# Own buffers for modulation tiles, a four-block start of an output projection, and moved gates in a two-layer hybrid decoder

## The chip, the cores and the metric

The kernel runs on one core of one Trainium2 chip. The metric is the device time of one execution in microseconds, the median of several runs. The engines are TensorE (PE: matmuls; PEld: their weight loads), VectorE (DVE), ScalarE (ACT), GpSimd (POOL) and SyncE (SP), whose queue issues the DMAs.

## The reference

A trunk of two layers runs over 256 tokens of width 2048, batch 1. Each layer has a token mixer and a squared-ReLU MLP (hidden width 8192), each behind an RMSNorm that is modulated by the conditioning vector c, and each added to the residual through a gate from c. Everything is float32.

```python
def ada_modulate(x, c, w, b):
    mod = jax.nn.silu(c) @ w + b                  # 2048 -> 3 * 2048
    shift, scale, gate = jnp.split(mod, 3, axis=-1)
    return rms_norm(x) * (1.0 + scale[:, None, :]) + shift[:, None, :], gate[:, None, :]

# layer 0, mLSTM: 8 heads, chunks of 128 tokens, hh = the heads' outputs (width 256 each)
    hh = hh * lax.rsqrt(jnp.mean(hh * hh, axis=-1, keepdims=True) + EPS)
    hh = hh.reshape(B, S, V_W) * norm_g
    y = (hh * jax.nn.sigmoid(o)) @ w_out
# layer 1, RG-LRU: xb, gb = split(h @ w_in); xb = conv4(xb) + conv_b; r, i = block-diagonal gates of xb
    log_a = -RG_C * r * jax.nn.softplus(-lam)
    u = jnp.sqrt(-jnp.expm1(2.0 * log_a)) * (i * xb)
    hs = scan(a=exp(log_a), u);  y = (hs * jax.nn.gelu(gb)) @ w_out
# both layers
    x = x + gate * y
    h, gate = ada_modulate(x, c, ada_w[layer, 1], ada_b[layer, 1])
    x = x + gate * (jnp.square(jax.nn.relu(h @ w1)) @ w2)
# end: rms_norm(x) * final_g
```

## The kernel before

**Layout and precision.** Activations lie transposed: 16 tiles of 128 features by 256 tokens. Weights come from HBM in tiles of 128 x 2048 (1 MB) through SP's queue into the pool `wpool` of four buffers (tag `raw`). `weights` splits each into a rounded part `whi` (two ACT copies of 1024 columns) and a rest `wlo` (two DVE subtractions); activations are split likewise by `pair`. A float32 product is then three passes of 256 columns: hi x hi, hi x lo, lo x hi. `mm3` issues them as three matmuls (L180 to L182), `mm2` as one of 512 columns and one of 256 (L186, L187); `block` makes one 128-wide output block from 16 of these.

**Modulation.** There are 4 x 48 modulation tiles of 128 x 2050 (1 MB). `ada_tile` loads one into a buffer of the same four (`adaraw`, tag `raw`) and one DVE instruction (L121) multiplies it by `cbc`, the broadcast of silu(c), and sums it. They are a filler: `fill`, called after a block, issues the next ones by a rate that `QKV_RATE` (in the first stage, by group) or `PACE` (later: how many are to be done at the end of a phase) gives; `need` issues what a step can't do without.

**First stage.** The sums of squares for the norm (`nsq` on ACT, `ss` on PE, L442) and the broadcast of c (`bc` on PE, L110, copied to `cbc` by ACT, L112) come first. The projections q, k, v and half of the output gate run over the 2048 inputs in five `GROUPS` of 2, 4, 4, 4 and 2 slices of 128, so that the first products need few modulation tiles; `group` (L489) adds each group to what lies in SBUF. Group 0's first tile `wdir` is used unsplit (float32, four passes a matmul). After group 0, `idle` issues 16 matmuls on ones (L522).

**mLSTM.** The stabiliser's rows go to DRAM and back as a broadcast (`rows_d`, `MB`). Eight heads follow, between the blocks of the other half of the output gate (`ogate`; `OB` says how many where). `state` makes the products cp (L636), `head` the head's output and denominator, keeps a copy `hb` and its square; `meansq` sums the square (L667). After each second head, `normed` takes the reciprocal root (L257 to L259) and multiplies `hb` by norm gain and root (L693), and `gated` multiplies by the gate, `(th + 1) * hb` (L700), and splits the result (`pair`, L171, L172). The output projection then is 16 `block`s over the 16 split tiles.

**The next norm.** While the residual is made, `unnormed` prepares rows for the next products ahead of the norm's root; `early_block` uses them and `scaled` applies the root afterwards (L203 to L205). `quad` makes four such blocks from four weight tiles.

**RG-LRU.** Per pair of blocks (n4) and for n = 0, 1 within it: the two xb blocks (unnormed if j < `MORE_RG`), convolution, the gates (`gacc`, split weights `ghi`, `glo`), tanh and exp on ACT, the two gb blocks; at the pair's end square root, gelu, the scan and y on ACT and DVE (L820 to L832). `modulated` makes the normed, split activations (`hmod`, L297; pairs L174, L175); here it stands at n = 1.

A scheduler sets the order of instructions on each engine from the program's order and its priorities; `high_priority` draws L121 forward.

Of the kernel before, what the change touches and what calls it, by code (L numbers as in the profile page):

```python
# [57 lines left out]
def trunk_kernel(ctx, tc, xT_d, par_d, ada_d, wqkv_d, wg_d, wo_d, awo_d, bwi_d, bg_d, bwo_d,  # L58
# [474 lines left out]
    with ExitStack() as mctx:  # L533
# [152 lines left out]

        def normed(h2, rs):
            rsqrt(rs, rs, 1.0, TINY)
            for i in range(2):
                for eb in range(2):  # L690
                    j = 4 * h2 + 2 * i + eb
                    t = hbs[2 * h2 + i][:, eb, :]
                    V.scalar_tensor_tensor(out=t, in0=t, scalar=halfg[:, j:j + 1], in1=rs[:, i, :],  # L693
                                           op0=ALU.mult, op1=ALU.mult)

        def gated(upto):
            while len(zs) < upto:
                j = len(zs)
                th = ths[j // 2][:, j % 2, :]
                V.scalar_tensor_tensor(out=th, in0=th, scalar=1.0, in1=hbs[j // 2][:, j % 2, :],  # L700
                                       op0=ALU.add, op1=ALU.mult)
                zs.append(pair(th))
# [218 lines left out]
```

## Time and profile before

| | us |
|---|---|
| median of 3 runs (2246.16 to 2250.83) | 2250.19 |
| the profiled execution | 2250.5 |
| its span | 2248.6 |
| busy: PE / DVE / ACT / POOL | 2192.2 / 1724.0 / 1287.5 / 86.0 |
| DMA: 601.27 MB, mean | 267 GB/s |

The page gives busy time for each engine, the chain of work that ended last, and groups of instructions by line. The trace adds windows (busy time, TensorE's granted clock, DMA share and rate in a stretch) and timelines (each instruction, and in brackets how long its engine had stood and what released it). A matmul on unsplit float32 operands leaves two records, so that the 16 sums of squares are `x32` in the timelines. "PE L522 MATMUL idle" are the matmuls of `idle`, not a gap.

### The profile page before, as it was taken

Reading aid. Unit: us, or ns where it says so; the run is one execution under the profiler, and the core shown is the slowest. Engines: PE = TensorE matmul, PEld = TensorE weight load, DVE = VectorE, ACT = ScalarE, POOL = GpSimd, SP = SyncE. Lnnn points to the kernel's source line nnn. Section 1 sums busy time; section 2 is a strip of 40 time slices with the busy share of each in tenths; the row PEclk is TensorE's granted clock in tenths of the full one; section 3 lists DMA queues with packets and bytes.
Section 4 is the critical chain, followed back from the end, with each engine's and each line's share of the span. In section 5 each row is a group of like instructions: output and inputs, shape, how many; then the busy total and the mean of one; then the engine's idle time right before and its main releaser. Section 6 shows DMA issues by size and latency. Waiting matters only on the chain.

```text
span 2248.6 us, 34262 instructions
## 1 busy us (share of the span) xinstructions
PE 2192.2 (97%) x13630; PEld 1965.7 (87%) x13630; DVE 1724.0 (77%) x2219; ACT 1287.5 (57%) x1997; POOL 86.0 (4%) x70
## 2 busy tenths in 40 slices
PE   7999998999999999999999899999999999999998
PEld 6899897998888888888889889889888889888887
DVE  5877789998997778888888998889875555555554
ACT  4777875445673336664444777756664334665443
POOL 0000010310000000000100000110000000000110
PEclk8999999999999999999999999999999999999999
DMA  8999877878778989898897577667875555555552
GB/s 326 332 335 340 317 285 292 324 294 316 280 283 319 332 321 342 306 329 322 318 335 268 200 243 266 223 207 263 306 282 198 188 187 188 187 188 187 188 189 93
DMA packets 88672, 601.27 MB, mean 267 GB/s; under 512 B 10424, under 2 KB 14648, under 8 KB 16192
## 3 DMA queue, kind: packets, MB, share of 16 engines
q1 hardware_dynamic: 86400, 598.03, 73.8%
q8 instruction: 107, 1.75, 0.3%
q10 hardware_dynamic: 2112, 1.05, 0.2%
q14 instruction: 53, 0.43, 0.1%
HBM read 596.93 MB, written 2.11 MB: 266 GB/s over the span
## 4 chain that ended last, share of the span: by engine, by line
PE 87%; DVE 6%; ACT 3%; issue 2%; DMA 2%; SPq 0%; DVEq 0%; ACTq 0%
PE mm L186 42%; PE mm L187 22%; PE mm L489 9%; PE mm L180 2%; PE mm L181 2%; PE mm L182 2%; DVE wlo L162 2%; PE mm L204 1%; PE mm L203 1%; DVE adaraw L121 1%; PE mm L205 1%; ACT whi L161 1%; DMA adaraw<-in_ada 1%; PE mm L343 0%; DMA MB<-rows_d 0%
## 5 line engine op out<-in xcount | busy, mean ns | idle before, releaser
L186 PE MATMUL mm<-pair,whi 128*128 128x512 f32 x4272 | 1500.9, 395 | 2.9 <-DVE pair L175 2.8
L162 DVE TENSOR_TENSOR wlo<-raw,whi 128x1024 fp32r<-128x1024 f32 x736 | 899.5, 1231 | 410.4 <-ACT whi L161 408.2
L187 PE MATMUL mm<-pair,wlo 128*128 128x256 f32 x4272 | 1198.8, 281 | 0.0
L161 ACT ACTIVATE whi<-raw 128x1024 fp32r<-128x1024 f32 x736 | 772.9, 1058 | 630.4 <-PE mm L186 505.6
L186 PEld LDWEIGHTS mm<-pair,whi 128*128 128x128 f32 x4272 | 803.8, 188 | 191.5 <-DVE pair L175 3.8
L187 PEld LDWEIGHTS mm<-pair,wlo 128*128 128x128 f32 x4272 | 806.6, 189 | 1.0 <-DVE wlo L162 0.3
L121 DVE SCALAR_TENSOR_TENSOR adaraw<-adaraw,cbc 128x2050 f32<-128x2050 f32 x192 | 439.0, 2288 | 41.2 <-DMA adaraw<-in_ada 29.7
L180 PE MATMUL mm<-pair,whi 128*128 128x256 f32 x720 | 206.3, 288 | 14.1 <-ACT pair L171 6.6
L182 PE MATMUL mm<-pair,wlo 128*128 128x256 f32 x720 | 205.6, 287 | 5.2 <-DVE wlo L162 5.2
L181 PE MATMUL mm<-pair,whi 128*128 128x256 f32 x720 | 205.8, 287 | 0.1
L180 PEld LDWEIGHTS mm<-pair,whi 128*128 128x128 f32 x720 | 139.3, 194 | 15.4 <-ACT pair L171 7.0
L182 PEld LDWEIGHTS mm<-pair,wlo 128*128 128x128 f32 x720 | 139.5, 194 | 5.9 <-DVE wlo L162 5.8
L181 PEld LDWEIGHTS mm<-pair,whi 128*128 128x128 f32 x720 | 139.3, 194 | 0.7 <-DVE pair L175 0.3
L489 PE MATMUL mm<-pair,whi 128*128 128x256 f32 x736 | 133.0, 284 | 4.5 <-ACT mm L504 2.9
L489 PEld LDWEIGHTS mm<-pair,whi 128*128 128x128 f32 x736 | 114.2, 190 | 5.7 <-ACT mm L504 3.1
L364 ACT ACTIVATE hsum<-hsum 128x256 f32<-128x256 f32 x121 | 49.2, 414 | 98.3 <-DVE hsum L247 87.8
L489 PE MATMUL mm<-pair,wlo 128*128 128x256 f32 x368 | 104.1, 283 | 0.7 <-DVE wlo L162 0.7
L322 DVE SCALAR_TENSOR_TENSOR xall<-mm,mod,xall 128x256 f32<-128x256 f32 x170 | 81.6, 481 | 27.8 <-PE mm L187 22.4
L277 POOL TENSOR_TENSOR nacc<-nacc,nsq 128x256 f32<-128x256 f32 x52 | 72.1, 1387 | 345.5 <-ACT nsq L268 335.2
L489 PE MATMUL mm<-whi,pair 128*128 128x512 f32 x256 | 82.9, 401 | 2.2 <-ACT whi L161 2.1
L489 PEld LDWEIGHTS mm<-pair,wlo 128*128 128x128 f32 x368 | 70.3, 191 | 1.3 <-DVE wlo L162 1.3
L203 PE MATMUL mm<-unnormed,whi 128*128 128x258 f32 x240 | 68.5, 285 | 0.0
(211 smaller groups left out, 1650.5 us busy)
## 6 DMA issues: line engine op xcount, KB each, us to landing
raw<-in_w SPq DMA_DIRECT2D x220, 1024.0 KB, 5.0
adaraw<-in_ada SPq DMA_DIRECT2D x192, 1025.0 KB, 6.3
raw<-in_wqkv SPq DMA_DIRECT2D x39, 1024.0 KB, 6.6
raw<-in_w1a SPq DMA_DIRECT2D x32, 1024.0 KB, 5.4
raw<-in_bwi SPq DMA_DIRECT2D x28, 1024.0 KB, 5.0
raw<-in_awo SPq DMA_DIRECT2D x16, 1024.0 KB, 5.5
raw<-in_bwo SPq DMA_DIRECT2D x16, 1024.0 KB, 5.2
raw<-in_wo SPq DMA_DIRECT2D x8, 1024.0 KB, 5.0
```

The source lines that it names most:

```text
L121: V.scalar_tensor_tensor(out=raw, in0=raw, scalar=1.0, in1=cbc, op0=ALU.mult, op1=ALU.mult, accum_out=mod[i][:, j:j + 1])
L161: A.activation(hi, sl, AF.Copy)
L162: V.tensor_tensor(out=lo, in0=sl, in1=hi.bitcast(F32), op=ALU.subtract)
L180: PE.matmul(out, lhsT=whi, rhs=p[:, 0, :], start=first, stop=False)
L181: PE.matmul(out, lhsT=whi, rhs=p[:, 1, :], start=False, stop=False)
L182: PE.matmul(out, lhsT=wlo, rhs=p[:, 0, :], start=False, stop=last)
L186: PE.matmul(out, lhsT=whi, rhs=p.rearrange("p a t -> p (a t)"), start=first, stop=False)
L187: PE.matmul(out[:, 0:S], lhsT=wlo, rhs=p[:, 0, :], start=False, stop=last)
L203: PE.matmul(out[:, 0:UX], lhsT=whi, rhs=u[:, 0:UX], start=first, stop=False)
L277: G.tensor_tensor(out=self.acc, in0=self.acc, in1=sq, op=ALU.add)
L322: V.scalar_tensor_tensor(out=xT[j], in0=acc[:, a:a + S], scalar=mod[i][:, 32 + j:33 + j], in1=xT[j], op0=ALU.mult, op1=ALU.add)
L489: PE.matmul(out, lhsT=l, rhs=m, start=clear and kk + n == 0, stop=kk == gn - 1 and n == len(ops) - 1, skip_group_check=True)
```

## The change

Six things change.

- Modulation tiles get a pool of their own of two buffers (`adax`) during groups 0 to 3; the first four alternate between it and `raw`. `QKV_RATE` goes from (1.6, 0.8, 0.8, 0.8, 1) to (1.6, 1, 1, 1, 1.2); `IDLE` from 16 to 4. `ACT_BUFS` goes from 46 to 44, `MLP_BUFS` from 6 to 8.
- The first sum of squares on PE keeps its place in the program, so the scheduler no longer draws four of the sums ahead of the broadcast.
- The first four blocks of the mLSTM's output projection run together over four quad tiles (`awoa`), kg = 0 to 3; heads 6 and 7 are kg = 3.
- The gate is multiplied in right after the head (`gated`), ahead of its norm; `hb` is scaled by the gain when ACT copies it; `normed` then multiplies 128 x 512 by the root and splits it.
- `MORE_RG` now counts n: the xb blocks j = 0 to 3 stay unnormed, and the gb blocks of n = 1 become unnormed too; `modulated` moves from n = 1 to n = 2.
- `PACE` changes in four phases.

```diff
-ACT_BUFS = 46
-MLP_BUFS = 6
+ACT_BUFS = 44
+MLP_BUFS = 8
-IDLE = 16
+IDLE = 4
+ADA_BUFS = 2
-MORE_RG = 4
+MORE_RG = 2
-QKV_RATE = (1.6, 0.8, 0.8, 0.8, 1)
-PACE = dict(o=52, out0=66, w1a=82, w1b=90, mlp0=160, mix1=174, out1=176, mlp1=192)
+QKV_RATE = (1.6, 1, 1, 1, 1.2)
+PACE = dict(o=54, out0=66, w1a=82, w1b=92, mlp0=168, mix1=170, out1=176, mlp1=192)
...
     def ada_tile(i, j):
-        raw = wpool.tile([P, ADA], F32, name="adaraw", tag="raw")
+        if adas and len(done) > 4 or len(done) % 2 < len(adas):
+            raw = adas[0].tile([P, ADA], F32, name="adaraw", tag="ada")
+        else:
+            raw = wpool.tile([P, ADA], F32, name="adaraw", tag="raw")
...
-    PE.matmul(ss, lhsT=ones, rhs=sq, start=j == 0, stop=j == KC - 1)
+    mm = PE.matmul(ss, lhsT=ones, rhs=sq, start=j == 0, stop=j == KC - 1)
+    if j == 0:
+        tc.keep_in_program_order(mm)
...
-    for gi in range(len(GROUPS) - 1):
-        group(gi, group_h(gi))
-        if gi == 0:
-            idle(IDLE, ob[-1][:, 0, :])
-    h32 = group_h(len(GROUPS) - 1)
+    with ExitStack() as actx:
+        adas.append(actx.enter_context(tc.tile_pool(name="adax", bufs=ADA_BUFS)))
+        for gi in range(len(GROUPS) - 1):
+            group(gi, group_h(gi))
+            if gi == 0:
+                idle(IDLE, ob[-1][:, 0, :])
+        h32 = group_h(len(GROUPS) - 1)
+        adas.clear()
...
-            A.activation(hbh, num, AF.Copy)
+            for eb in range(2):
+                A.activation(hbh[:, eb, :], num[:, eb, :], AF.Copy,
+                             scale=halfg[:, 2 * h + eb:2 * h + eb + 1])
...
+        def gated():
+
+            while len(ts) < len(hbs) and 2 * len(ts) + 2 <= obs[0]:
+                h = len(ts)
+                V.scalar_tensor_tensor(out=ths[h], in0=ths[h], scalar=1.0, in1=hbs[h], op0=ALU.add,
+                                       op1=ALU.mult)
+                ts.append(ths[h])
+
         def normed(h2, rs):
+
             rsqrt(rs, rs, 1.0, TINY)
             for i in range(2):
+                t = ts[2 * h2 + i]
+                V.tensor_tensor(out=t, in0=t, in1=rs[:, i, :].unsqueeze(1).broadcast_to([P, 2, S]),
+                                op=ALU.mult)
+                hi = act.tile([P, 2, S], F32R, name="zhi", tag="act")
+                lo = act.tile([P, 2, S], F32R, name="zlo", tag="act")
+                A.activation(hi, t, AF.Copy)
+                V.tensor_tensor(out=lo, in0=t, in1=hi.bitcast(F32), op=ALU.subtract)
...
+        accs = [ps.tile([P, S], F32, name="mm") for _ in range(4)]
+        for kg in range(4):
+            w = weights(awoa_d[kg])
+            for kk in range(4):
+                hi, lo = w[kk // 2]
+                for b in range(4):
+                    o = kk % 2 * 512 + b * P
+                    mm3(accs[b], hi[:, o:o + P], lo[:, o:o + P], zs[kg * 4 + kk], kg + kk == 0,
+                        kg + kk == 6)
         for j in range(KC):
-            acc = block([awo_d[j]], zs, mm3)
+            acc = accs[j] if j < 4 else block([awo_d[j]], zs, mm3)
...
-                if n == 1:
+                if n == MORE_RG:
                     hs += [modulated(2, j, r) for j in range(KC)]
...
-                    if n == 0:
-                        _, c = scaled(accs[2 + d], r, gb[:, d, :])
+                    if n < MORE_RG:
+                        acc = accs[2 + d] if n == 0 else early_block(bwi_d[16 + 2 * n + d], us)
+                        _, c = scaled(acc, r, gb[:, d, :])
```

PE's queue at the start of the program, before. `ss` are the norm's sums, `bc` the broadcast of c, `hdirect` the first modulated tiles.

```order
L442 MATMUL ss<-nsq,ones 128x256 x4
L110 MATMUL bc<-ident,sc 128x128 x16
L442 MATMUL ss<-nsq,ones 128x256 x12
L489 MATMUL mm<-hdirect,wdir 128x256 x16
L489 MATMUL mm<-pair,whi 128x256 x2
```

The same place in the changed kernel.

```order
L112 MATMUL bc<-ident,sc 128x128 x16
L449 MATMUL ss<-nsq,ones 128x256 x16
L498 MATMUL mm<-hdirect,wdir 128x256 x16
L498 MATMUL mm<-pair,whi 128x256 x2
L498 MATMUL mm<-pair,wlo 128x256
```

The broadcast now stands ahead of all sums.

DVE's queue after the last head's mean square (the first row), before: root, norm gain, gate and split of heads 6 and 7, with modulation tiles (`adaraw`) and weight splits (`wlo`) between.

```order
L668 SCALAR_TENSOR_TENSOR rs<-hss,em 128x256
L257 SCALAR_TENSOR_TENSOR rsu<-rs,rsy 128x512
L121 SCALAR_TENSOR_TENSOR adaraw,mod_128<-adaraw,cbc 128x2050
L162 TENSOR_TENSOR wlo<-raw,whi 128x1024
L258 SCALAR_TENSOR_TENSOR rsu<-rsu,rsy 128x512
L121 SCALAR_TENSOR_TENSOR adaraw,mod_128<-adaraw,cbc 128x2050
L259 SCALAR_TENSOR_TENSOR rs<-rsu,rsy 128x512
L693 SCALAR_TENSOR_TENSOR hb_3563<-hb_3563,halfg,rs 128x256 x2
L693 SCALAR_TENSOR_TENSOR hb_3676<-hb_3676,halfg,rs 128x256 x2
L700 SCALAR_TENSOR_TENSOR th<-th,hb_3563 128x256 x2
L700 SCALAR_TENSOR_TENSOR th<-th,hb_3676 128x256
L172 TENSOR_TENSOR pair<-th,pair 128x256 x3
```

The same place in the changed kernel.

```order
L682 SCALAR_TENSOR_TENSOR rs<-hss,em 128x256
L126 SCALAR_TENSOR_TENSOR adaraw,mod_128<-adaraw,cbc 128x2050
L168 TENSOR_TENSOR wlo<-raw,whi 128x1024 x2
L264 SCALAR_TENSOR_TENSOR rsu<-rs,rsy 128x512
L265 SCALAR_TENSOR_TENSOR rsu<-rsu,rsy 128x512
L168 TENSOR_TENSOR wlo<-raw,whi 128x1024
L266 SCALAR_TENSOR_TENSOR rs<-rsu,rsy 128x512
L126 SCALAR_TENSOR_TENSOR adaraw,mod_128<-adaraw,cbc 128x2050
L714 TENSOR_TENSOR th<-th,rs 128x512 x2
L168 TENSOR_TENSOR wlo<-raw,whi 128x1024
L719 TENSOR_TENSOR zlo<-th,zhi 128x512
```

The gain and gate steps are gone from here (the gate's L705 stands earlier), and a multiplication and a split of 128 x 512 for each head remain.

ACT's queue in the second mixer, from the end of the tanh and exp of n = 0 on, before. `pair<-hmod` are the modulated activations, `TT` becomes the square root, `gb` goes through the gelu.

```order
L803 ACTIVATE TT<-th,sp_11570 128x256
L814 ACTIVATE gb<-gb,shc 128x256 x2
L767 ACTIVATE ghi<-graw 128x512
L161 ACTIVATE whi<-raw 128x1024
L767 ACTIVATE ghi<-graw 128x512
L821 ACT_TABLE_LOAD
L821 ACTIVATE TT<-TT 128x512
L174 ACTIVATE pair<-hmod,mod_129 128x256 x8
L823 ACT_TABLE_LOAD
L823 ACTIVATE gb<-gb 128x512
```

The changed kernel, from the end of the tanh and exp of n = 1 on, one n later than in the rows above.

```order
L828 ACTIVATE TT<-th,sp_11562 128x256
L167 ACTIVATE whi<-raw 128x1024
L840 ACTIVATE gb<-gb,shc 128x256 x2
L847 ACT_TABLE_LOAD
L847 ACTIVATE TT<-TT 128x512
L849 ACT_TABLE_LOAD
L849 ACTIVATE gb<-gb 128x512
L177 ACTIVATE pair<-gb 128x256 x4
L792 ACTIVATE ghi<-graw 128x512 x2
L180 ACTIVATE pair<-hmod,mod_129 128x256 x11
```

The modulated pairs now stand behind the gelu and the pairs of y.

## Rows read from the trace of the kernel before

**Rows 1.** The page: busy time of the engines, the chain's shares, two groups of DVE.

```profile
PE 2192.2 (97%) x13630; PEld 1965.7 (87%) x13630; DVE 1724.0 (77%) x2219; ACT 1287.5 (57%) x1997; POOL 86.0 (4%) x70
...
PE 87%; DVE 6%; ACT 3%; issue 2%; DMA 2%; SPq 0%; DVEq 0%; ACTq 0%
...
L162 DVE TENSOR_TENSOR wlo<-raw,whi 128x1024 fp32r<-128x1024 f32 x736 | 899.5, 1231 | 410.4 <-ACT whi L161 408.2
...
L121 DVE SCALAR_TENSOR_TENSOR adaraw<-adaraw,cbc 128x2050 f32<-128x2050 f32 x192 | 439.0, 2288 | 41.2 <-DMA adaraw<-in_ada 29.7
```

**Rows 2.** Windows (us): busy per engine (instructions), TensorE's clock, DMA share, GB/s.

```profile
100.00:150.00 50.00, 50.00 (x346) 46.31 (x345) 39.90 (x39) 39.75 (x57) 0.00 (x0) 1.00 0.92 331
...
200.00:250.00 50.00, 50.00 (x319) 45.00 (x318) 38.36 (x36) 37.03 (x53) 0.00 (x0) 1.00 0.91 336
...
350.00:400.00 50.00, 40.83 (x280) 38.45 (x279) 46.78 (x69) 24.57 (x45) 0.54 (x1) 0.86 0.80 294
...
400.00:450.00 50.00, 46.22 (x379) 46.01 (x379) 49.00 (x59) 24.81 (x45) 18.28 (x10) 0.97 0.92 338
...
1200.00:1250.00 50.00, 43.53 (x342) 42.38 (x342) 42.38 (x83) 31.80 (x50) 0.00 (x0) 0.93 0.63 229
```

**Rows 3.** Windows of other lengths, same columns.

```profile
30.00:35.00 5.00, 5.00 (x21) 4.25 (x21) 1.40 (x3) 2.89 (x5) 0.00 (x0) 0.87 0.62 218
...
65.00:70.00 5.00, 4.20 (x25) 3.69 (x24) 3.51 (x5) 5.00 (x9) 0.00 (x0) 1.00 1.05 366
...
435.00:480.00 45.00, 45.00 (x382) 44.95 (x382) 43.70 (x41) 18.86 (x25) 15.08 (x7) 1.00 0.98 370
...
395.00:400.00 5.00, 5.00 (x25) 5.00 (x25) 4.96 (x8) 0.79 (x3) 0.00 (x0) 0.51 0.50 166
```

**Rows 4.** Timeline of PE, start to group 3: start, duration, operation, [idle before <-releaser].

```profile
5.80 3.78 PE L442 MATMUL ss<-nsq,ones 128*128 128x256 f32 x8 [5.80 <-ACT nsq L441]
...
25.66 2.93 PE L489 MATMUL mm<-hdirect,wdir 128*128 128x256 f32 x6 [6.68 <-ACT hdirect L302]
...
67.11 7.17 PE L522 MATMUL idle<-th,ones 128*128 128x256 f32 x32 [0.80 <-ACT th L515]
...
242.71 0.28 PE L489 MATMUL mm<-pair,wlo 128*128 128x256 f32 x1
```

**Rows 5.** Timeline of DVE at the start: the first modulation tile.

```profile
14.47 2.29 DVE L121 SCALAR_TENSOR_TENSOR adaraw<-adaraw,cbc 128x2050 f32<-128x2050 f32 x1 [11.04 <-ACT cbc L112]
```

**Rows 6.** Timeline of PE, heads 5 to 7 and the first out-projection blocks.

```profile
364.93 0.28 PE L180 MATMUL mm<-pair,whi 128*128 128x256 f32 x1
...
366.12 0.28 PE L181 MATMUL mm<-pair,whi 128*128 128x256 f32 x1
...
368.50 0.50 PE L180 MATMUL mm<-pair,whi 128*128 128x256 f32 x2 [2.11 <-ACT pair L171]
...
378.42 0.59 PE L667 MATMUL hss<-hsq,ones 128*128 128x256 f32 x2
...
394.28 0.80 PE L180 MATMUL mm<-pair,whi 128*128 128x256 f32 x2 [4.47 <-ACT pair L171]
```

**Rows 7.** Timeline of DVE, norm and gate of heads 6 and 7.

```profile
391.76 1.67 DVE L693 SCALAR_TENSOR_TENSOR hb<-hb,halfg,rs 128x256 f32<-128x256 f32 x4
...
393.35 1.09 DVE L700 SCALAR_TENSOR_TENSOR th<-th,hb 128x256 f32<-128x256 f32 x3
```

**Rows 8.** Timeline of PE, a later out-projection block.

```profile
429.41 0.39 PE L182 MATMUL mm<-pair,wlo 128*128 128x256 f32 x1 [3.79 <-DVE wlo L162]
```

**Rows 9.** Timeline of PE, the gap in the second mixer.

```profile
1247.47 0.80 PE L180 MATMUL mm<-pair,whi 128*128 128x256 f32 x2 [6.47 <-ACT pair L174]
```

**Rows 10.** Timeline of ACT in that gap.

```profile
1246.39 0.63 ACT L821 ACTIVATE TT<-TT 128x512 f32<-128x512 f32 x1
...
1246.93 3.29 ACT L174 ACTIVATE pair<-hmod,mod 128x256 fp32r<-128x256 f32 x8
...
1250.23 1.28 ACT L823 ACT_TABLE_LOAD   x1
```

More of the change, by code (lines that the diff above doesn't have):

```diff
@@ L122, in ada_tile @@
                                    accum_out=mod[i][:, j:j + 1])
+    adas = []
     filler = []
@@ L179, in mm3 @@
     def mm3(out, whi, wlo, p, first, last):
-        PE.matmul(out, lhsT=whi, rhs=p[:, 0, :], start=first, stop=False)
-        PE.matmul(out, lhsT=whi, rhs=p[:, 1, :], start=False, stop=False)
-        PE.matmul(out, lhsT=wlo, rhs=p[:, 0, :], start=False, stop=last)
+        hi, lo = p if isinstance(p, tuple) else (p[:, 0, :], p[:, 1, :])
+        PE.matmul(out, lhsT=whi, rhs=hi, start=first, stop=False)
+        PE.matmul(out, lhsT=whi, rhs=lo, start=False, stop=False)
+        PE.matmul(out, lhsT=wlo, rhs=hi, start=False, stop=last)
     def mm2(out, whi, wlo, p, first, last):
@@ L668, in meansq @@
             V.scalar_tensor_tensor(out=out, in0=ss, scalar=1.0 / DV, in1=em, op0=ALU.mult, op1=ALU.add)
-        hbs, zs = [], []
+        hbs, ts, zs = [], [], []
         obs = [OG]
@@ L689, in normed @@
             for i in range(2):
-                for eb in range(2):
[L691 to L702, printed above, removed]
+                t = ts[2 * h2 + i]
[5 more added lines that the diff above has]
+                V.tensor_tensor(out=lo, in0=t, in1=hi.bitcast(F32), op=ALU.subtract)
+                for eb in range(2):
+                    zs.append((hi[:, eb, :], lo[:, eb, :]))
         pace("o", 16 - OG)
@@ L714, in trunk_kernel @@
             hbs.append(hbh)
+            gated()
             if h + 1 < H:
@@ L720, in trunk_kernel @@
                 normed(h // 2, rs)
-                gated(min(2 * h + 2, obs[0]))
-        for _ in range(16 - obs[0]):
-            ogate(1)
-            gated(obs[0])
         norm, us = Norm(), []
         pace("out0", 14)
+        accs = [ps.tile([P, S], F32, name="mm") for _ in range(4)]
[7 more added lines that the diff above has]
+                        kg + kk == 6)
         for j in range(KC):
-            acc = block([awo_d[j]], zs, mm3)
+            acc = accs[j] if j < 4 else block([awo_d[j]], zs, mm3)
             residual(0, j, acc, norm, us, KC // 2)
@@ L770, in trunk_kernel @@
                 xf, xp = [], []
-                if n == 1:
+                if n == MORE_RG:
                     hs += [modulated(2, j, r) for j in range(KC)]
                 for j in (2 * n, 2 * n + 1):
-                    if j < MORE_RG:
-                        acc, c = scaled(accs[j] if j < 2 else early_block(bwi_d[j], us), r)
+                    if n < MORE_RG:
+                        acc, c = scaled(accs[j] if n == 0 else early_block(bwi_d[j], us), r)
                         A.activation(acc, acc, AF.Identity, bias=c)
@@ L811, in trunk_kernel @@
                 for d in range(2):
-                    if n == 0:
-                        _, c = scaled(accs[2 + d], r, gb[:, d, :])
+                    if n < MORE_RG:
+                        acc = accs[2 + d] if n == 0 else early_block(bwi_d[16 + 2 * n + d], us)
+                        _, c = scaled(acc, r, gb[:, d, :])
                         A.activation(gb[:, d, :], gb[:, d, :], AF.Identity, bias=c)
@@ L896 @@
         "wo": cols(w_in[:, 4096 + OG * P:6144]),
+        "awoa": quads(a["a_w_out"][0][:, 0:512]),
         "awo": cols(a["a_w_out"][0]),
```

2 lines of the change are left out of this document (1 added, 1 removed).

## The prediction

> **What bounds the kernel now.** I read the engines' busy time and the chain first [rows 1]: TensorE is busy for 97% of the span and is 87% of the chain of work that ended last, DVE 6% of it. So time can only come out of the places where TensorE stands or runs at half clock, and out of the beginning and end. The windows of 50 us show where these places are [rows 2]: from 100 to 250 us TensorE is busy without a gap; 350 to 400 has only 40.83 us of work at a mean clock of 0.86, 400 to 450 has 46.22, 1200 to 1250 has 43.53. The start has the rest: the first projection matmul begins at 25.66, and at 67.11 TensorE runs, for 7.17 us, 32 records of idle matmuls that fill a wait [rows 4]. Next I read what stands before each gap, and what the DMA does there [rows 3], since the first edit is one of transfers. A unit below is a matmul pass of 256 columns: ten of them lie between 364.93 and 366.12, so 0.119 us each at full clock [rows 6].
>
> The profiled execution took 2250.5 us (span 2248.6), 0.3 us above the median of 2250.19; I sum against the 2250.5.
>
> **Start and projection groups 0 to 3.** The modulation tiles leave the four shared weight buffers, and the broadcast of c goes ahead of the norm's sums on TensorE. Now DVE waits 11.04 us and begins its first tile at 14.47, behind a broadcast that stands behind four of sixteen sums, 3.78 us of TensorE; then four tiles (2.29 each) and the norm's three steps stand ahead of the first product [rows 1, 4, 5]. The broadcast can end some 4 us earlier; the fourth tile's landing then bounds, so I give the first matmul 3 us. With own buffers the weights of group 0 no longer wait behind a consumed modulation tile: from 30 to 35 us the DMA moved only 218 GB/s [rows 3]. The idle matmuls shrink from 16 to 4; a record pair takes 7.17 / 16 = 0.45 us, so 12 of them are 5.4 us [rows 4], but they stand in a wait, and are worth something only if the weights of group 1 come as early. I read the order for what must come: up to the 36th weight tile, near the end of group 3, the queue now carries 36 modulation tiles and then 42, so 6 more of 1.05 MB, 6.3 MB.
>
> That decides this stage. From 50 us to the last matmul of group 3 at 242.71 [rows 4] the DMA moved 64.3 MB at 331 to 336 GB/s and 0.91 to 0.92 of its share, with TensorE full [rows 2]. The thirty weight tiles from 74 us on take 169 us, 5.63 us each; one weight and one modulation tile in 5.63 us are 373 GB/s. The trace shows 370 over 435 to 480, and 366 in 65 to 70, both at a share near 1 [rows 3]; 336 / 0.92 is 365. So the stage turns from TensorE's to the DMA's. With 1 MB more moved before 50 us, the 64.3 + 6.3 - 1.0 = 69.6 MB at 366 take 190 us and end at 240.2: gain 2.6. At 336, as now, they take 207 us and end at 257 (loss 14); however fast the DMA, TensorE's 169 us bind, and from 64 us, 10 before now, they end at 233 (gain 10). I take 366, as the longest full stretch is nearest to it: **+2.6, from -14 to +10**.
>
> A page of the Trainium skill, "DMA: Bandwidth & Descriptors" (section "Where 436 GB/s comes from"), speaks against the edit: it puts the limit of HBM for one NeuronCore at about 358 GB/s, though its measured table has 425 for one core alone with 16 MB. The trace has 370 over 45 us, so it is above that limit here; by 358 the 69.6 MB would take 194 us, and this term would be -1.6.
>
> **Around the first head.** The modulation rate in the last group rises to 1.2, which asks for more than the DMA's 370 there too; I put **-1** on it (-3 to 0). Of the output-gate blocks that cover the first head's stabiliser (a round trip through DRAM), the order shows 64 units between the k products and the first state product where 112 stood: 48 x 0.119 = 5.7 us of cover go [rows 6]. No wait stood there before. DVE has 6 weight splits ahead of it in that place where 8 stood, at 1.23 each [rows 1], which gives back 2.4 if DVE ends that chain, and nothing if the round trip does. So 3.3 to 5.7 us where the old cover was just enough, 0 where it was ample, and -7 with the lower clock behind a gap; I take **-4**.
>
> **Heads 6, 7 and the first projection blocks.** In 350 to 400 us TensorE stands 50 - 40.83 = 9.2 us: 2.11 before 368.50 and 4.47 before 394.28, both for the split of gated head outputs on ACT, and three smaller waits [rows 2, 6]. Behind the large one it runs at 0.51 of its clock up to 400, the lower of its two levels, with 25 matmuls in 5 us where 435 to 480 has 42 [rows 3]; with the same behind the first gap, the mean of 0.86 [rows 2] stands for 14 us at half clock, some 10 of them busy, so about 5 us more, 14 together. The chain that releases it starts with the last mean square at 378.42 and ends with the pairs after 394.28, 15.9 us, and in it DVE runs four normalising steps (1.67) and three gate steps (1.09) in a row behind modulation tiles [rows 6, 7]. Afterwards the gate is already in, so two multiplications of 512 columns take their place: about 1.4 by halves of 1.67 and 1.09, hence a chain of some 14 us. In the order 117 units of the four-block product, with heads 0 to 5 alone, stand between that mean square and the first use of head 6: 117 x 0.119 = 13.9 us of cover. I walked DVE's queue there: two modulation tiles, four splits, the norm, the multiplications; the first half is ready at about 13.4 of 13.7, the second some 0.5 late. Gain **+13**; if a modulation tile lands late, 4 us of wait and as much again of clock come back: +6 is the low end, 14 the high one.
>
> What is late next is the fifth to eighth block. Now 3.79 us go at 429.41, for weight splits queued behind modulation tiles on DVE [rows 8]; with two fewer fills in the phase the order still shows a weight tile issued behind a modulation tile that must be consumed first. I take **+2** (-3 to +3). Two more MLP buffers and two more fills per phase hide under a full TensorE (500 us on): -0.5.
>
> **Second mixer.** Before 1247.47 TensorE idles 6.47 us for the first modulated pairs [rows 9]. The change brings two more early blocks (2 x 48 units are only moved; the sum of work is the same) and defers the modulated pairs to n = 2. So behind the last early matmul ACT now has, ahead of the first pair, what stood behind it: a table load (1.28), the gelu (as the square root, 0.63), four pairs of y (0.41 each) and two gate-weight copies (0.63 each), 4.8 us, and DVE's y steps between them, about 1 us more [rows 10]. The gap grows to about 12.4, -5.9; later small waits lose their modulation tiles, +1.4. Term **-4.5**; if the y steps overlap with the square root's wait it stays at 6.5 (+2), at worst it is -8.
>
> **Sum:** 2.6 - 1 - 4 + 13 + 2 - 0.5 - 4.5 = +7.6, so 2250.5 - 7.6 = **2243**.
>
> **The rivals.** *Slower:* the QKV stage becomes the DMA's. All other terms sum to +5, so this decides from the rate: below 69.6 MB / (252.3 - 50) = 344 GB/s the kernel is over 4.5 us slower; at today's 336 it is 2250.5 - 5 + 14 = 2260. For it: 331 to 336 is all that this mix of tiles has shown for 150 us; against it: the share of 0.92 there [rows 2, 3]. *No change:* the rate lies between 344 and 360, or the heads give only 6 because DVE is late for head 7: 2246 to 2254, the middle about 2250. For it: 13.4 of 13.7 us is no margin. By the page's 358 GB/s the time would be here as well, 2250.5 - 3.4 = 2247. *Faster than forecast:* the mixer's gap does not grow and the stage runs at 370: 2250.5 - 5 - 6.5 - 4.7 = 2234; for it, that DVE has room while ACT loads tables. *Not what it says:* the gate's step could stay behind the norm; the order excludes it, since each gate step stands ahead of its head's mean square.
>
> **How the numbers follow.** A measurement of this kernel tells 0.2%, 4.5 us, from no change. Forecast (2238 to 2245.5) 0.38; faster than that 0.14; no change 0.26; slower 0.22. So faster 0.52, same 0.26, slower 0.22. The range leaves out a tenth on each side: from 2229 (366 to 370 GB/s, no loss at the stabiliser, no growth in the mixer) to 2258 (about 338 GB/s with the other terms as they are).
>
> **What would show it.** Right: from 80 to 230 us a DMA share near 1 at 360 to 370 GB/s, with TensorE just below 50 of 50; group 3 ending near 240; no idle over 1 us before the first matmul that reads zhi of head 6; TensorE over 48 of 50 in 350 to 400; one gap of 10 to 13 us in the second mixer, with pairs of y on ACT ahead of it. Wrong: a projection stage under 350 GB/s or with gaps of several us per group; a wait for zhi with half clock behind it; a gap of more than 7 us at the first state product; or a mixer gap of 6 us or less.

## The result and the profile after

The changed kernel takes 2271.72 us, median of four runs (2270.35 to 2275.47), against 2250.51 for the kernel before in the same comparison: a ratio of 1.0099, 95% interval 1.0079 to 1.0119. It is 21 us slower, and outside the predicted range of 2229 to 2258.

The kernel before was measured again beside each set of runs below, with medians from 2247.7 to 2250.5 us; so a difference of 2 to 3 us between runs of different sets says little by itself, and the traces must tell it.

The engines' busy time on the page of the changed kernel looks almost like that before [rows 1]: TensorE is as busy, in a span that is 21 us longer.

```profile
PE 2191.2 (97%) x13606; PEld 1955.9 (86%) x13606; DVE 1719.1 (76%) x2199; ACT 1279.8 (56%) x1997; POOL 84.4 (4%) x70
```

Windows of the changed kernel (busy time of PE, PEld, DVE, ACT, POOL, TensorE's clock, DMA share, GB/s), to be read against [rows 2]:

```profile
100.00:150.00 50.00, 46.08 (x303) 40.23 (x302) 38.10 (x38) 31.81 (x49) 0.00 (x0) 1.00 0.86 320
...
200.00:250.00 50.00, 46.20 (x279) 38.97 (x277) 34.80 (x31) 32.14 (x47) 0.00 (x0) 1.00 0.86 318
...
350.00:400.00 50.00, 49.96 (x400) 48.48 (x399) 40.19 (x57) 36.50 (x65) 1.81 (x3) 1.00 0.58 201
...
400.00:450.00 50.00, 44.89 (x359) 44.08 (x359) 49.22 (x63) 22.15 (x42) 14.09 (x8) 0.97 0.92 334
...
1250.00:1300.00 50.00, 37.89 (x265) 35.35 (x265) 43.38 (x93) 42.14 (x72) 0.00 (x0) 0.86 0.34 121
```

The stretch that had no gap, 100 to 250 us, now has 46 of 50 us busy, and the DMA moves less there than before, 318 to 320 GB/s at a share of 0.86. The stretch of the heads, 350 to 400, is full. Of 1250 to 1300, where the second mixer's gap now lies, 12 us are idle.

The same places in the program in both kernels, from the timelines of PE, give a balance (start of the first matmul there; the loss is the growth of the stretch that ends there):

| place | before | after | loss of the stretch |
|---|---|---|---|
| first projection matmul | 25.66 | 25.19 | -0.5 |
| first matmul of group 1 | 73.93 | 65.64 | -7.8 |
| last matmul of group 3 | 242.71 | 261.78 | +27.4 |
| first state product (cp) | 296.28 | 315.32 | 0.0; 5.7 at equal work |
| first full block of the first MLP | 488.44 | 499.94 | -7.5; -13.2 at equal work |
| its last three-pass block | 1190.38 | 1207.57 | +5.7 |
| last three-pass block of the second mixer | 1508.46 | 1530.09 | +4.4 |
| the last norm sum | 2239.66 | 2260.88 | -0.4 |

"At equal work" allows for 48 units, 5.7 us, of output-gate blocks that the change moves from ahead of the first state product to behind it. A three-pass block is one made by `mm3`. The sum is 21.2 us. The largest loss by far, 27.4 us, more than the whole, is in the thirty tiles of groups 1 to 3. A step there, the time for one weight tile, took (242.71 - 73.93) / 30 = 5.63 us before and (261.78 - 65.64) / 30 = 6.54 after.

Three rows of PE's timeline in the changed kernel, to be read against [rows 4]: the first product, the idle matmuls that end group 0, the last matmul of group 3.

```profile
25.19 3.35 PE L498 MATMUL mm<-hdirect,wdir 128*128 128x256 f32 x7 [8.36 <-ACT hdirect L309]
...
64.00 1.99 PE L531 MATMUL idle<-th,ones 128*128 128x256 f32 x8 [0.79 <-ACT th L524]
...
261.78 0.28 PE L498 MATMUL mm<-pair,wlo 128*128 128x256 f32 x1
```

### The profile page after: what moved, and what is told of

Read it like the earlier page. It is cut to its first block, busy times and chain, and to the rows that moved or that the text cites. A ratio compares the mean times of both kernels' runs of the same rounds, so it can differ in the third digit from the quotient of the medians.

```text
span 2269.9 us, 34176 instructions
## 1 busy us (share of the span) xinstructions
PE 2191.2 (97%) x13606; PEld 1955.9 (86%) x13606; DVE 1719.1 (76%) x2199; ACT 1279.8 (56%) x1997; POOL 84.4 (4%) x70
## 4 chain that ended last, share of the span: by engine, by line
PE 73%; DVE 3%; ACT 1%; issue 1%; DVEq 0%; ACTq 0%
PE mm L193 42%; PE mm L194 22%; PE mm L211 1%; PE mm L210 1%; PE mm L212 1%; PE mm L188 1%; PE mm L187 1%; PE mm L189 1%; DVE wlo L168 1%; DVE adaraw L126 1%; PE mm L350 0%; ACT whi L167 0%; PE gacc L187 0%; PE gacc L188 0%; PE gacc L189 0%
## 5 line engine op out<-in xcount | busy, mean ns | idle before, releaser
L194 PE MATMUL mm<-pair,wlo 128*128 128x256 f32 x4272 | 1197.2, 281 | 8.8 <-DVE wlo L168 8.8
L193 PEld LDWEIGHTS mm<-pair,whi 128*128 128x128 f32 x4272 | 802.8, 188 | 203.9 <-issue 12.3
L194 PEld LDWEIGHTS mm<-pair,wlo 128*128 128x128 f32 x4272 | 804.8, 188 | 12.3 <-DVE wlo L168 11.8
L498 PE MATMUL mm<-pair,whi 128*128 128x256 f32 x736 | 136.3, 288 | 8.5 <-ACT mm L513 4.6
L498 PEld LDWEIGHTS mm<-pair,whi 128*128 128x128 f32 x736 | 114.4, 193 | 12.4 <-ACT whi L167 5.7
L188 PE MATMUL mm<-pair,whi 128*128 128x256 f32 x432 | 122.1, 283 | 0.0
L187 PE MATMUL mm<-pair,whi 128*128 128x256 f32 x432 | 121.9, 282 | 0.0
L189 PE MATMUL mm<-pair,wlo 128*128 128x256 f32 x432 | 121.6, 281 | 0.0
L498 PE MATMUL mm<-pair,wlo 128*128 128x256 f32 x368 | 104.0, 291 | 8.1 <-DVE wlo L168 7.8
L187 PEld LDWEIGHTS mm<-pair,whi 128*128 128x128 f32 x432 | 81.5, 189 | 0.4
L189 PEld LDWEIGHTS mm<-pair,wlo 128*128 128x128 f32 x432 | 81.6, 189 | 0.2 <-DVE wlo L168 0.2
L188 PEld LDWEIGHTS mm<-pair,whi 128*128 128x128 f32 x432 | 81.5, 189 | 0.0
L498 PEld LDWEIGHTS mm<-pair,wlo 128*128 128x128 f32 x368 | 70.1, 194 | 12.0 <-DVE wlo L168 12.0
L210 PE MATMUL mm<-unnormed,whi 128*128 128x258 f32 x272 | 77.4, 285 | 0.0
```

The costliest lines, as they stand in the source:

```text
L187: PE.matmul(out, lhsT=whi, rhs=hi, start=first, stop=False)
L188: PE.matmul(out, lhsT=whi, rhs=lo, start=False, stop=False)
L189: PE.matmul(out, lhsT=wlo, rhs=hi, start=False, stop=last)
L193: PE.matmul(out, lhsT=whi, rhs=p.rearrange("p a t -> p (a t)"), start=first, stop=False)
L194: PE.matmul(out[:, 0:S], lhsT=wlo, rhs=p[:, 0, :], start=False, stop=last)
L210: PE.matmul(out[:, 0:UX], lhsT=whi, rhs=u[:, 0:UX], start=first, stop=False)
```

## The experiments

**What limits the step in groups 1 to 3.** SP's waits in the changed kernel, 100 to 250 us (total, times, longest), point at the two own buffers: SP stands for 129.7 of 150 us until DVE has consumed a modulation tile, and the weight tiles stand behind on its queue.

```profile
SPq L124 <- DVE adaraw L126: 129.7, 23, 6.0
```

So the first theory was a loop through these buffers; a third one should break it (run e1).

```diff
-ACT_BUFS = 44
-MLP_BUFS = 8
-ADA_BUFS = 2
+ACT_BUFS = 40
+MLP_BUFS = 12
+ADA_BUFS = 3
```

> Changed kernel with three buffers for modulation tiles in groups 0 to 3 instead of two; to make room ACT_BUFS is 40 instead of 44 and MLP_BUFS 12 instead of 8. Theory L (a loop through the two buffers: a modulation tile holds its buffer for 12.9 us from its issue to the end of its DVE instruction, and the next weight tile stands behind the next modulation tile on SP's queue, so two buffers give 6.4 us a step): with three, 12.9 / 3 = 4.3 us no longer binds, the steps go back to 5.63 to 5.8 us, the DMA rises from 318 to 360 GB/s or more in 100 to 250 us, group 3 ends at 240 to 246 us instead of 261.5, and the kernel takes 2250 to 2257. Theory B (the DMA cannot bring two tiles a step faster than 318 GB/s): the steps stay at 6.4 us, group 3 ends after 257, and the kernel takes 2266 to 2272.

Measured: 2274.94 us, ratio 1.0109 (1.0091 to 1.0127) to the kernel before, as slow as the changed kernel, 3 us above what theory B gave. The step is 6.54 us again. The windows from 100 to 230 us, of the changed kernel and then of this one, agree to 0.02 us of TensorE's busy time. SP waits nearly as long as ever: in the row below 116.2 of the 140 us from 100 to 240; from 100 to 230 it is 110.7 us here and 113.2 in the changed kernel.

```profile
100.00:230.00 130.00, 119.17 (x763) 102.82 (x762) 96.41 (x94) 83.90 (x126) 0.00 (x0) 1.00 0.85 318
```

```profile
100.00:230.00 130.00, 119.19 (x763) 102.81 (x762) 96.38 (x94) 83.94 (x126) 0.00 (x0) 1.00 0.85 317
```

```profile
SPq L124 <- DVE adaraw L126: 116.2, 21, 6.0
```

The theory falls. A third buffer, as we read it, is only filled one step earlier and then waits as well: SP's wait would be a sign that the DMA is ahead, not that it is late. But this run alone also fits a DMA that gives no more than 318 GB/s.

The next run (e2) undoes the modulation part of the first stage: shared buffers, old rates, 16 idle matmuls. The broadcast ahead of the sums stays.

```diff
-        adas.append(actx.enter_context(tc.tile_pool(name="adax", bufs=ADA_BUFS)))
-QKV_RATE = (1.6, 1, 1, 1, 1.2)
-IDLE = 4
+QKV_RATE = (1.6, 0.8, 0.8, 0.8, 1)
+IDLE = 16
```

> Changed kernel with the first stage as before: modulation tiles in the shared buffers, the old rates of groups 0 to 4, 16 idle matmuls. If the first stage alone carries the 19 us between group 3's end at 242.7 and 261.5, that end is back at 240 to 243 and the kernel takes 2250 to 2256 (the six modulation tiles then fall to the heads, which may cost up to 4). If the late end is made up later by having six tiles done early, the kernel stays above 2262.

Measured: 2246.44 us, ratio 0.999 (0.998 to 0.9999), 4 us below the expected range. Group 3 ends at 239.24, the step is 5.63 us again, TensorE has no gap from 100 to 230 us:

```profile
100.00:230.00 130.00, 130.00 (x853) 118.40 (x852) 101.19 (x99) 102.10 (x148) 0.00 (x0) 1.00 0.91 332
```

Undoing this part gives back 25 us, more than the loss of the whole change; 22.5 of them are there by the end of group 3 (261.78 to 239.24).

The timelines of the changed kernel show what a step waits for. First PE, twice a split weight `wlo`, 6.39 us apart:

```profile
158.74 0.50 PE L498 MATMUL mm<-wlo,pair 128*128 128x512 f32 x1 [0.53 <-DVE wlo L168]
...
165.13 0.50 PE L498 MATMUL mm<-wlo,pair 128*128 128x512 f32 x1 [0.53 <-DVE wlo L168]
```

Then ACT and DVE in between:

```profile
161.60 0.60 ACT L524 ACTIVATE v<-mm 128x512 f32<-128x512 f32 x1 [1.73 <-PE mm L498]
...
162.23 0.60 ACT L513 ACTIVATE mm<-v 128x512 f32<-128x512 f32 x1
...
162.77 1.99 ACT L167 ACTIVATE whi<-raw 128x1024 fp32r<-128x1024 f32 x2
```

```profile
163.85 2.36 DVE L168 TENSOR_TENSOR wlo<-raw,whi 128x1024 fp32r<-128x1024 f32 x2 [1.29 <-ACT whi L167]
```

ACT stands 1.73 us for PE to end the first accumulator of the present tile, copies it out (161.60), fills the next accumulator (162.23), and only then splits the next weight tile (162.77), though no wait of that split on a DMA shows; DVE follows 1.1 us behind it, and its first half ends near 165.0, when PE goes on. From 161.60 to 165.13 are 3.5 us, and PE's half tile before is 2.8 (half of 5.63): 6.3 together, the step. In the kernel before ACT has the same work in another order (its timeline in the same stretch): it waits 0.16 and 0.33 us for PE (there are four split buffers, and PE must let go of one), splits, and copies out afterwards.

```profile
157.42 1.06 ACT L161 ACTIVATE whi<-raw 128x1024 fp32r<-128x1024 f32 x1 [0.16 <-PE mm L489]
...
158.81 1.06 ACT L161 ACTIVATE whi<-raw 128x1024 fp32r<-128x1024 f32 x1 [0.33 <-PE mm L489]
...
159.78 0.58 ACT L515 ACTIVATE v<-mm 128x512 f32<-128x512 f32 x1
```

The order of instructions on ACT tells it without any time. Tile by tile, v2 and v3 come from one weight tile, v4 and v5 from the next, v6 and v7 from the one behind; `whi_929` and `whi_926` split the tile of v6 and v7. The fills of accumulators and the pairs of activations between are left out. Before:

```
L161 ACTIVATE whi_929<-raw_927 128x1024
L161 ACTIVATE whi_933<-raw_927 128x1024
L515 ACTIVATE v3_198<-mm_869 128x512
...
L515 ACTIVATE v4_199<-mm_894 128x512
```

Changed:

```
L524 ACTIVATE v3_198<-mm_863 128x512
...
L524 ACTIVATE v4_199<-mm_891 128x512
...
L167 ACTIVATE whi_926<-raw_924 128x1024
L167 ACTIVATE whi_930<-raw_924 128x1024
L524 ACTIVATE v5_200<-mm_906 128x512
```

Before, the split of the tile two ahead stands ahead of the second copy-out of the present tile; in the changed kernel it is the tile one ahead. One tile of lead is gone, and with it the slack between PE, ACT's copy, ACT's split, DVE's split and PE. To test this alone, run e6 pins the order as before in the changed kernel, with its transfers, rates and buffers:

```diff
+                w = ahead.pop(nt, None) or weights(wqkv_d[nt])
...
-                    A.activation(dst, acc, AF.Copy)
+                    if gi in (1, 2, 3) and t == 1 and c0 + 512 == width and nt + 1 < 36:
+                        ahead[nt + 1] = weights(wqkv_d[nt + 1])
+                        last[:] = split
+                    with tc.issue_after(last[0].ins) if last else nullcontext():
+                        last[:] = [A.activation(dst, acc, AF.Copy)]
```

`split` holds the last split on ACT; `issue_after` sets the order on the queue and adds no wait. From weight tile 8 to 33 SP's queue has its transfers, and DVE's its splits and modulation tiles, in the same sequence as in the changed kernel; what moves is ACT's order.

> Changed kernel in which only an order is pinned in groups 1 to 3: ACT splits the weight tile two ahead before it copies out the second accumulator of the present tile, as in the kernel before (in the changed kernel the split one tile ahead stands there). Transfers, rates and buffers are those of the changed kernel. Theory O (the scheduler's order puts each split one tile later, so that PE, ACT's copy, ACT's split, DVE's split and PE form a loop of 6.4 us a step): the steps go back to 5.63 to 5.85, the first stage's DMA rises from 318 to 355 or more, group 3 ends at 236 to 246 us, the kernel takes 2248 to 2257. Theory B (the DMA delivers no more): steps stay at 6.3 or above, the kernel takes 2266 or more.

Measured: 2246.77 us, ratio 0.9994 (0.9981 to 1.0006), 25 us less than the changed kernel and 1 below the expected range. The step is (235.53 - 65.40) / 30 = 5.67 us, group 3 ends at 235.53, and from 100 to 230 us TensorE has no gap while the DMA moves 370 GB/s:

```profile
100.00:230.00 130.00, 130.00 (x868) 119.05 (x867) 113.27 (x110) 96.32 (x145) 0.00 (x0) 1.00 0.95 370
```

ACT's timeline now has splits ahead of the copies, and one that waits for the DMA, 0.23 us:

```profile
156.47 2.01 ACT L171 ACTIVATE whi<-raw 128x1024 fp32r<-128x1024 f32 x2 [0.23 <-DMA raw<-in_wqkv]
...
158.39 0.57 ACT L534 ACTIVATE v<-mm 128x512 f32<-128x512 f32 x1
...
160.22 0.60 ACT L534 ACTIVATE v<-mm 128x512 f32<-128x512 f32 x1 [1.25 <-PE mm L504]
```

The order is the cause, and the DMA does bring a weight and a modulation tile in every step. SP waits for a modulation tile to be consumed here too, 115.0 of the 150 us from 100 to 250, with TensorE full: its wait is no sign of a loss. Two further runs tell which edit gave that order. One (e7) keeps the own buffers and takes the old rates, the other (e8) takes the kernel before with the new rates alone.

```diff
-QKV_RATE = (1.6, 1, 1, 1, 1.2)
+QKV_RATE = (1.6, 0.8, 0.8, 0.8, 1)
```

> Changed kernel with the old modulation rates (1.6, 0.8, 0.8, 0.8, 1) in the first stage, own buffers and 4 idle matmuls kept. In its order the split of the tile two ahead stands behind the second copy-out of the present tile, half a tile later than in the kernel before and half a tile earlier than in the changed one. Theory O: a loop of half a tile more slack no longer binds; steps of 5.63 to 5.8 us, group 3 ends at 236 to 243, the kernel takes 2244 to 2252. If the buffers are the cause and not the rate: steps stay above 6.2, the kernel takes 2262 or more.

```diff
-QKV_RATE = (1.6, 0.8, 0.8, 0.8, 1)
+QKV_RATE = (1.6, 1, 1, 1, 1.2)
```

> Kernel before with the new modulation rates (1.6, 1, 1, 1, 1.2) alone; shared buffers. Its order loses the lead of the splits step by step and has that of the changed kernel from about the seventh tile on. Theory O: steps of 6.3 us or more from about 90 us on, group 3 ends at 255 to 262, the kernel takes 2258 to 2268 (six modulation tiles fewer later give some back). If the rate alone is harmless: group 3 ends before 248, the kernel takes 2245 to 2253.

Measured: 2251.3 us, ratio 1.0015 (1.0005 to 1.0024), with the own buffers and the old rates; 2263.01, ratio 1.0063 (1.005 to 1.0077), with the new rates alone. The windows from 100 to 230 us, in that order:

```profile
100.00:230.00 130.00, 129.15 (x842) 116.89 (x841) 100.72 (x98) 96.88 (x143) 0.00 (x0) 1.00 0.84 324
```

```profile
100.00:230.00 130.00, 120.50 (x772) 104.84 (x771) 98.16 (x94) 84.53 (x128) 0.00 (x0) 1.00 0.88 320
```

With the old rates the step is 5.76 us; with the new rates on shared buffers it is 6.31, and group 3 ends at 264.04, 2 us later than was expected. So the rate turns the order, in either layout of the buffers; the buffers by themselves cost 0.1 us a step at the old rates (5.76 after 5.63 in e2). Why the scheduler sets a split later when a modulation tile goes with every weight tile was not tried; only its order was seen.

**The first MLP.** Its rows in the changed kernel show six waits of 0.62 to 1.48 us for `wlo` between 808 and 1163 us that the kernel before does not have, 6.4 us in sum. One of them, on PE:

```profile
1082.61 0.38 PE L194 MATMUL mm<-pair,wlo 128*128 128x256 f32 x1 [1.48 <-DVE wlo L168]
```

And DVE ahead of it:

```profile
1073.86 2.28 DVE L126 SCALAR_TENSOR_TENSOR adaraw<-adaraw,cbc 128x2050 f32<-128x2050 f32 x1
...
1076.15 2.28 DVE L126 SCALAR_TENSOR_TENSOR adaraw<-adaraw,cbc 128x2050 f32<-128x2050 f32 x1
...
1080.94 0.48 DVE L329 SCALAR_TENSOR_TENSOR xall<-mm,mod,xall 128x256 f32<-128x256 f32 x1 [2.50 <-PE mm L194]
...
1081.34 2.35 DVE L168 TENSOR_TENSOR wlo<-raw,whi 128x1024 fp32r<-128x1024 f32 x2
```

DVE has two modulation tiles in a row, then stands 2.50 us at a residual step that waits for PE's block, with the split behind it: the tile for the next block is there, its split is late. The paces of the later phases are put back (e3):

```diff
-PACE = dict(o=54, out0=66, w1a=82, w1b=92, mlp0=168, mix1=170, out1=176, mlp1=192)
+PACE = dict(o=54, out0=66, w1a=82, w1b=90, mlp0=160, mix1=174, out1=176, mlp1=192)
```

> Changed kernel with the paces of the later phases as before (w1b 90, mlp0 160, mix1 174 instead of 92, 168, 170). Theory F (the eight more fills put modulation tiles ahead of weight splits on DVE, seen as waits of 0.5 to 1.5 us in the first MLP that sum to some 8 us): those waits go, the stretch from the first MLP's start to its last out block shrinks by 5 to 6, the kernel takes 2265 to 2268, less 1 to 2 given back in the mixer. Theory M (the buffer counts 44 and 8 changed the order, not the paces): the waits stay and the kernel takes 2270 to 2273.

Measured: 2268.96 us, 2.8 less than the changed kernel, less than the spread of either's executions and 1 above the expected 2268 at most. The trace is plainer: the six waits are gone; the gap in the second mixer, which has fourteen modulation tiles again, is longer than in the changed kernel, 15.57 us after 12.11, and gives half back:

```profile
1282.37 0.76 PE L193 MATMUL mm<-pair,whi 128*128 128x512 f32 x1 [15.57 <-DVE pair L181]
```

**The second mixer.** PE's gap in the changed kernel, to be read against [rows 9], and ACT ahead of it, against [rows 10]:

```profile
1285.41 0.77 PE L193 MATMUL mm<-pair,whi 128*128 128x512 f32 x1 [12.11 <-DVE pair L181]
```

```profile
1279.58 0.63 ACT L849 ACTIVATE gb<-gb 128x512 f32<-128x512 f32 x1
...
1280.12 0.70 ACT L177 ACTIVATE pair<-gb 128x256 fp32r<-128x256 f32 x2
...
1281.27 0.42 ACT L177 ACTIVATE pair<-gb 128x256 fp32r<-128x256 f32 x1 [0.45 <-DVE gb L857]
...
1282.61 0.42 ACT L177 ACTIVATE pair<-gb 128x256 fp32r<-128x256 f32 x1 [0.93 <-DVE gb L857]
...
1282.93 1.13 ACT L792 ACTIVATE ghi<-graw 128x512 fp32r<-128x512 f32 x2
...
1283.97 3.29 ACT L180 ACTIVATE pair<-hmod,mod 128x256 fp32r<-128x256 f32 x8
```

Ahead of the eight modulated pairs at 1283.97 stand the gelu, the pairs of y, two of which wait 0.45 and 0.93 us for DVE's product, and the gate weights. The mixer's edit is undone, the rest stays (e4):

```diff
-MORE_RG = 2
+MORE_RG = 4
...
-                if n == MORE_RG:
+                if n == 1:
...
-                    if n < MORE_RG:
+                    if n == 0:
```

> Changed kernel with the second mixer as before (four early xb blocks counted by block, the gate blocks of n = 0 alone early, modulated pairs at n = 1). Theory G (the deferred pairs stand behind the gelu and the pairs of y on ACT): the gap of 12.1 us before the first modulated pairs goes back to about 6.5, and the kernel takes 2266 to 2269. Rival: with two modulation tiles instead of fourteen in the mixer the old order had its own late split, and the gap is only moved: 2271 to 2273.

Measured: 2264.18 us, 7.5 less, 2 below the expected range. The gap is 4.15 us, shorter than in the kernel before as well, which has fourteen modulation tiles in this phase where this one has two:

```profile
1263.28 0.80 PE L187 MATMUL mm<-pair,whi 128*128 128x256 f32 x2 [4.15 <-ACT pair L180]
```

That the tiles make this difference is seen in e3 against the changed kernel, and in e5 below, which has the old order with fourteen of them, and the old gap (6.47 in [rows 9]):

```profile
1228.90 0.79 PE L187 MATMUL mm<-pair,whi 128*128 128x256 f32 x2 [6.48 <-ACT pair L180]
```

So the new order costs 12.11 - 4.15 = 8.0 us in the gap with two tiles, and 15.57 - 6.48 = 9.1 with fourteen.

**The heads.** With the first stage, the later paces and the mixer as before, only the heads' edit is left, with the broadcast ahead of the sums, the buffer counts and the pace of the phase `o` (run e5).

> Kernel before plus the edits at the heads: first stage, the paces of the first MLP and the second mixer, and the mixer's order are as before; gate ahead of the norm, four projection blocks at once, the broadcast ahead of the sums, the buffer counts 44 and 8 stay. If the three undone parts add up as measured one by one (19 us lost in the first stage; 6 in the first MLP against 2 in the mixer; 8 in the mixer's gap) and the heads keep their 13 of gain less what the first head's stabiliser costs, the kernel takes 2234 to 2240. If the parts hide one another it takes over 2243.

Measured in five rounds: 2235.18 us, ratio 0.9936 (0.9922 to 0.995). It is faster than both kernels, by 0.6% against the one before. Its trace is of the fastest of five executions, 4.7 us below their median. The heads' edit doesn't carry all of the gain: group 1 begins at 71.62 where 73.93 stood, 2.3 us earlier. Its windows of 350 to 400 and 400 to 450 us, against 40.83 and 46.22 in [rows 2]:

```profile
350.00:400.00 50.00, 47.22 (x387) 46.20 (x385) 48.97 (x64) 30.76 (x57) 5.59 (x5) 1.00 0.81 293
...
400.00:450.00 50.00, 47.74 (x384) 46.90 (x382) 49.16 (x55) 23.20 (x33) 16.83 (x9) 0.97 0.95 359
```

The last run (e9) puts the pinned order, and with it the full rate of the first stage, under the same kernel; its edits are those of e6, e3 and e4.

> Changed kernel with the pinned order of e6 in groups 1 to 3, and the old mixer and old later paces of e3 and e4: all six more modulation tiles are done in the first stage at the new rate. If the parts add as before (e6's 2247 less 8 for the mixer's gap and less about 3 for the paces), the kernel takes 2234 to 2239, level with e5, so that a first stage that runs at 370 GB/s is worth nothing over the old rate once the heads are mended. If the six tiles done early are worth their DVE time at the heads as well, it takes 2228 to 2232.

Measured in five rounds: 2235.14 us, ratio 0.9938 (0.9924 to 0.9952), the same as without. Group 3 ends at 235.90, 4.5 us earlier than with the heads' edit alone (240.40), but the first state product comes at 296.64 after 291.40. PE waits right behind group 3 for a split that the pinned order does not reach (e6, with the same first stage, has 3.02 there):

```profile
239.27 0.50 PE L197 MATMUL mm<-pair,whi 128*128 128x512 f32 x1 [3.09 <-ACT whi L171]
```

The windows from group 3's end to the first state product, of e5 and then of e9, and five microseconds of e9 behind its next wait (3.33 at the last group's entry) tell the rest:

```profile
240.40:291.40 51.00, 47.77 (x333) 43.63 (x331) 44.66 (x59) 42.61 (x71) 0.00 (x0) 1.00 0.85 304
```

```profile
235.90:296.64 60.74, 53.50 (x347) 48.98 (x346) 49.87 (x64) 46.10 (x75) 0.00 (x0) 0.92 0.83 303
```

```profile
260.00:265.00 5.00, 5.00 (x25) 5.00 (x25) 3.98 (x4) 2.95 (x5) 0.00 (x0) 0.50 0.76 302
```

The stretch is 9.7 us longer. TensorE stands for 7.2 us in it where it stood for 3.2; fourteen more matmuls are 1.7 us at 0.119; and the granted clock is 0.92 on average, down to 0.50, the lower of its two levels, behind the wait, which by 53.50 x 0.08 is an estimated 4.3 us. So the pinned order loses at its own end what it gains, and these runs do not show what a first stage without that wait would be worth.

## Why the prediction was wrong, step by step

**The start was right in size.** Group 1 begins 8.3 us earlier, where about 10 was the bound. The 3 us at the first product were not there, only 0.5: DVE now waits for the modulation tiles themselves (rows of DVE in the changed kernel: the first, second and fourth tile), so their landing binds, as the prediction said of the fourth tile, but 2.5 us later than it took.

```profile
12.25 2.30 DVE L126 SCALAR_TENSOR_TENSOR adaraw<-adaraw,cbc 128x2050 f32<-128x2050 f32 x1 [8.79 <-DMA adaraw<-in_ada]
...
15.47 2.29 DVE L126 SCALAR_TENSOR_TENSOR adaraw<-adaraw,cbc 128x2050 f32<-128x2050 f32 x1 [0.92 <-DMA adaraw<-in_ada]
...
20.45 2.29 DVE L126 SCALAR_TENSOR_TENSOR adaraw<-adaraw,cbc 128x2050 f32<-128x2050 f32 x1 [0.18 <-DMA adaraw<-in_ada]
```

**The step of groups 1 to 3 is where it failed.** The prediction put a step between two bounds, TensorE's 5.63 us and the DMA's 5.7, and took the stage for the DMA's. It never asked what stands between a landed tile and the first matmul on it, and so put ACT's split and its place in the queue at nothing. The step was 6.54. The rival called *slower* had this place, and its threshold of 344 GB/s was even passed (318), but its mechanism was wrong: the rate was low because tiles lay in full buffers. With the order held (e6), the term would have been 242.71 - 235.53 = +7.2, better than the +2.6 forecast. From 50 us to group 3's end the DMA of e6 moved 365 GB/s, as priced, and with that 67.7 MB where 69.6 were reckoned. But the stage did not turn from TensorE's to the DMA's: TensorE is busy for 130.00 of 130 us, and what the DMA could give at most no run shows. (The prediction's check, 336 / 0.92 = 365, takes the share of another row; the row of 336 has 0.91, which gives 369.) The mistake could have been seen before the run: the order of ACT's instructions shows the split one tile later. The 358 GB/s of the Trainium skill ("DMA: Bandwidth & Descriptors", section "Where 436 GB/s comes from"), by which the term would have been -1.6, did not bind on this one core: e6 holds 370 for 130 us.

**Around the first head: right in size, half right in cause.** 1 and 4 were forecast, 5.7 came: two waits at the last group's entry, where the kernel before has one of 2.91, and one of 2.05 at the first state product, where it has none. The -4 stands on the cover, and that holds: the three traces with 298 or 299 matmuls between group 3's end and the first state product wait there (the changed kernel 2.05 us, e7 1.79, e8 2.02); those with 333 or 347 do not (the kernel before, e2, e5, e6, e9). But e8 has none of the edits at the heads: the cover went with the order of the first stage, not with the four-block product. The -1 was put on a DMA asked for too much by the rate of 1.2; both waits end with ACT filling an accumulator, and e7, at the old rate of 1, has the same two (3.40 and 1.24). PE's timeline of the changed kernel:

```profile
277.54 0.50 PE L498 MATMUL mm<-pair,whi 128*128 128x256 f32 x2 [3.40 <-ACT mm L513]
...
280.92 0.79 PE L498 MATMUL mm<-pair,whi 128*128 128x256 f32 x2 [1.24 <-ACT mm L513]
...
315.32 0.70 PE L648 MATMUL cp<-v,kw 128*128 128x256 f32 x2 [2.05 <-ACT kw L630]
...
406.89 0.73 PE L187 MATMUL mm<-zhi,whi 128*128 128x256 f32 x4 [0.51 <-ACT zhi L718]
...
435.02 0.39 PE L189 MATMUL mm<-zhi,wlo 128*128 128x256 f32 x1 [4.18 <-DVE wlo L168]
```

**The heads: right.** The last two rows above are the first use of head 6, a wait of 0.51, and the wait in a later block, 4.18 where 3.79 stood [rows 8]. 13 and 2 were forecast, 13.2 came in sum: the wait in the later block was not shortened, so the +2 was not there. TensorE's 49.96 of 50 us from 350 to 400, at a clock of 1.00 where 0.86 stood, are what the prediction named as its sign.

**The first MLP: the second failed step.** "Hide under a full TensorE" was forecast at 0.5 and cost 5.7. Eight more fills are small against DVE's free time, but two of them together stand ahead of a split whose place in the queue is behind a residual step, and DVE, with 2.28 us each, has no room for that inside one block. Here a full TensorE did not hide what stood ahead of a split.

**The second mixer: the cause right, the size by luck.** A gap of 12.4 was forecast, 12.11 came; the term was 4.5, and 4.4 came. The pairs of y and the gelu do stand ahead on ACT. But two errors cancel: the order was put at 5.9 us and costs 8.0 in the gap, and the fewer modulation tiles, priced at 1.4 in later small waits, shorten the gap itself, from 6.48 to 4.15 in the old order and from 15.57 to 12.11 in the new.

So the sum, +7.6 forecast and -21.2 on the balance above, failed by 28.8 us: 21.7 in the first stage (+2.6 forecast, -19.1 came), 5.2 in the MLP, 1.8 at the heads, and 0.1 in all the rest together.

## What to carry to other kernels

The time of a busy engine and that of a transfer bound a pipeline's step from below; what sets it may be the order in which an engine between them alternates "copy out the old" with "prepare the new". Read that order for the lead of the preparing step, in tiles, before and after any change that moves other work into the same stage, even if the change touches no instruction of the pipeline itself. And a long wait of the queue that issues transfers need not mean a loss: here it said that buffers were full, with the same wait in a slow stage (e1) and in one with TensorE full (e6), and a further buffer gave nothing. When a forecast comes true in one place, look whether two terms cancelled, as in the mixer.

## What the runs showed of the hardware

One core moved 370 GB/s over 130 us at a DMA share of 0.95, with TensorE busy without a gap and DVE busy for 113 of the 130 us (e6); so the 318 to 320 GB/s of the same mix in the changed kernel and e8 were not the DMA's limit. A moved order of splits and copies on ACT is worth 0.9 us a step here, and 25 us in the kernel. Behind waits of about 3 us TensorE ran at 0.50 of its clock, the lower of its two levels, from 260 to 265 us in e9 and from 280 to 285 in the changed kernel; in e5, with a wait of 2.90 us, it stayed at 1.00.
